# Row norms applied in the transposes by a diagonal, and low parts taken from PSUM, in a one-core hybrid attention and recurrence step

## The chip, the core and the metric

The kernel runs on one core of a Trainium2 chip, as one launch. The core has five engines that run at once, each with its own queue of instructions, and wait for each other by semaphores: TensorE (PE, matrix products, whose weight loads the profile lists apart as PEld), VectorE (DVE), ScalarE (ACT), GpSimd (POOL) and SyncE (SP, which issues most DMAs here). Matrix products take both operands from the on-chip memory SBUF and write to the accumulation memory PSUM, from which only DVE and ACT read in this kernel.

The metric is the device time of one execution in microseconds (us). "The time before" is the median of three runs.

## The reference

One layer of a diffusion backbone, on 1024 latent tokens and 256 context tokens of width 1024, in float32:

```python
def rms_norm(x, w):
    xf = x.astype(F32)
    y = xf * lax.rsqrt(jnp.mean(xf * xf, axis=-1, keepdims=True) + EPS)
    return (y * w.astype(F32)).astype(x.dtype)

def one_block(qi):                      # in block_attention
    s = jnp.einsum('bqkgd,bskd->bkgqs', qi, kf) * scale
    p = jax.nn.softmax(s, axis=-1)
    return jnp.einsum('bkgqs,bskd->bqkgd', p, vf)

def trunk_layer(x, mod, norm_mix_w, mix_w, ffn_w, ctx_k, ctx_v, s0_fwd, s0_bwd, latent):
    sh1, sc1, g1, sh2, sc2, g2 = mod
    h = rms_norm(x, norm_mix_w) * (1.0 + sc1) + sh1
    out, k, v, s = token_mixer(h, *mix_w, ctx_k, ctx_v, s0_fwd, s0_bwd, latent)
    x = x + g1 * out
    norm_ffn_w, w_ff1, w_ff2 = ffn_w
    h = rms_norm(x, norm_ffn_w) * (1.0 + sc2) + sh2
    x = x + g2 * (jnp.square(jax.nn.relu(h @ w_ff1)) @ w_ff2)
    return x, k, v, s
```

`token_mixer` multiplies `h` by `w_in` (1024 x 5376), runs attention (8 heads of 64, 2 key heads; latents attend to 1024 latent and 512 cached keys, context to itself) and a gated linear recurrence forward and backward (4 heads, chunks of 32), gates and merges the two and multiplies by `w_out`. Three places divide or multiply whole rows by one number for each row: the first RMSNorm, the softmax's sum, and the second RMSNorm. They are what the change touches.

## The kernel before

Tokens come in three tiles: t = 0 and 1 are the latents (512 each, four blocks of 128 rows), t = 2 is the context (256, two blocks). To keep float32 precision at the fast product rate, most operands are split into a high part (rounded to the reduced type float32r, by ACT) and a low part (the rest, by DVE), and a product is three fast ones: high x high, high x low, low x high (`mm3` L319 to L321, `z_tok` L336 to L338). Some products are ordinary float32 matmuls without a split, those of the recurrence among them (L1083, L1095, L1114, L1116).

The stages follow each other:

1. *Start* (up to about 100 us). `norm1_rows` (L229) loads rows, sums their squares, takes the reciprocal root (`rst`) and scales the rows in place (`scale`, L253, on DVE). `norm1_tr` (L259) transposes 128x128 blocks on PE with the identity into PSUM; `norm1_col` (L271 to L277) applies the modulation, which by now is one scale `sc` and one shift `sh` for each partition, and writes the high part `hi` (ACT) and the low part `lo` (DVE), by way of `xnb`. For every third column of t < 2 `xnb` is computed by DVE (L274), else by ACT (L276).
2. *Attention* (about 160 to 710 us), 32 units of 256 latent queries of one head with 1536 keys (6 steps each) and 8 of the context with 256 keys (1 step). A unit's `score` (L819) makes scores of 128 queries x 512 keys, `expo` (L830) the exponentials `pexp` and their sums, whose reciprocal is `rs` (L834), `norm` (L838) multiplies `pexp` by `rs`, turn about on POOL and DVE (`NORM`), `trans` (L860) transposes four 128x128 blocks of `pexp` into one PSUM tile, from which ACT takes the high part `pTh` and DVE the low part `pTl` (L863), and `value` (L874, L875) multiplies them by the values. `events` sets the order by due times in steps of a unit, and between events `fill` puts products of `w_in` (a `Filler`) on PE in proportion.
3. *Recurrence* (about 710 to 1010 us), `hgrn`: 24 units, each with `prep` (scans and scalings on DVE and POOL), `keys_t` (transposes, L1072), `scores` (L1083), `states_` (L1095), `out` (L1114, L1116). Products of `w_in` fill PE here as well. The columns of the modulation are made on the way: `ada_cols` (L176) multiplies, copies the result to SBUF (`ev`, L178), and leaves a rest `late` in a list `todo`: a transpose (L182), a sum `adas` (L185) and an addition (L186). The rest is run when the next group of `w_in` products has begun.
4. *Projections* (about 1010 to 1320 us). The outputs of both branches are projected, gated and merged, multiplied by `w_out`, and added to the rows `xrow`. `out_norm` (L1385) stores the rows, computes their norm and scales them in place on DVE; `norm2_t` (L1393) transposes them on PE.
5. *MLP* (the rest).

What sets the order: PE's instructions stand as the code writes them; on DVE, ACT, POOL and SP a scheduler orders them by its own estimate, with `tc.high_priority` and `tc.issue_after(x)` ("not before x in the order") as hints. On each engine instructions then run strictly in that order. Buffers come from rings by name (`RING_OF`): a ring's next tile waits for the readers of the one that had the buffer. The ring "K" has one buffer, which holds `ident0` at the start and `R`, a constant of the recurrence's scans, later.

## Time and profile before

| | |
|---|---|
| median of three runs | 2056.77 us (2056.67 to 2057.38) |
| profiled execution, its own time | 2056.44 us |
| its span in the profile | 2054.7 us |
| granted TensorE clock, mean | 0.998 |
| DVE busy | 1407.0 us, 68% |
| ACT busy | 941.1 us, 46% |
| POOL busy | 533.1 us, 26% |

How to read the rows of the profile: a row of a group has line, engine, operation, the tile written, the tiles read (for a product the moving one first), the shapes and the number of records; then the busy time, the mean duration in ns, and the idle time of the engine just before, with what ended it. In a row of the timeline stand start, duration of the merged instructions, engine, line, operation, tiles, shapes and count, and in brackets the idle time before and its releaser. A matmul's duration is its latency; matmuls overlap, so what one costs is read from starts. L12 is line 12 of the kernel.

### The profile page before, as it was taken

To read this page: it belongs to the slowest core of one execution; us is meant where nothing else is said; L and a number is where in the kernel's file an instruction comes from. 1 tells how busy PE (TensorE), PEld (TensorE's weight loads), DVE (VectorE), ACT (ScalarE), POOL (GpSimd) and SP (SyncE) were. 2 spreads that over 40 slices of the span, in tenths; PEclk is the share of its full clock that TensorE was granted. 3 is DMA by queue.
4 is the path that set the end of the run, shared out by engine and by line. 5 is a ranking of instruction groups with operands and counts; after the bars stand their busy time and mean duration, and the time that the engine had idled before them with its cause. 6 is when DMAs were issued, how large, how long until landed. Compare 5 with 4: busy or idle time off the path is not lost.

```text
span 2054.7 us, 33792 instructions
## 1 busy us (share of the span) xinstructions
PE 2013.7 (98%) x12470; PEld 1735.2 (84%) x12470; DVE 1407.0 (68%) x2733; ACT 941.1 (46%) x1973; POOL 533.1 (26%) x526
## 2 busy tenths in 40 slices
PE   7899999999999999999999999999999999999998
PEld 5698889988889978888888889988888888888886
DVE  5866776767776788879254635886666666577686
ACT  4634555555555423333321335755455544333443
POOL 1452233333333355545112101222122110000120
PEclk9999999999999999999999999999999999999999
DMA  9452220321212454554644533854444489455764
GB/s 318 160 189 78 70 83 32 104 88 55 77 50 80 132 176 158 165 168 158 199 136 149 179 113 119 253 184 152 159 146 157 145 292 361 147 160 175 232 238 142
DMA packets 220612, 317.38 MB, mean 154 GB/s; under 512 B 18760, under 2 KB 139808, under 8 KB 220448
## 3 DMA queue, kind: packets, MB, share of 16 engines
q1 hardware_dynamic: 207968, 275.32, 41.8%
q0 software_dynamic: 12480, 39.91, 5.2%
q8 instruction: 98, 1.61, 0.3%
q14 instruction: 66, 0.54, 0.1%
HBM read 229.43 MB, written 85.74 MB: 153 GB/s over the span
## 4 chain that ended last, share of the span: by engine, by line
PE 87%; DVE 6%; DMA 3%; ACT 2%; issue 1%; SPq 0%; POOL 0%; POOLq 0%; DVEq 0%; ACTq 0%
PE ps_g L319 8%; PE ps_g L321 7%; PE ps_g L320 7%; PE ps_s L819 4%; PE ps_t L860 4%; PE ps_g L1749 2%; PE ps_g L1748 2%; PE ps_g L1750 2%; PE ps_s L1593 2%; PE ps_s L1594 2%; PE ps_s L1595 2%; PE ps_g L875 2%; PE ps_s L1748 2%; PE ps_s L1749 2%; PE ps_s L1750 2%; PE ps_g L336 2%
## 5 line engine op out<-in xcount | busy, mean ns | idle before, releaser
L319 PE MATMUL ps_g<-hs,wsp 128*128 128x512 f32 (+1 forms) x896 | 322.5, 360 | 4.0 <-DVE adas L185 4.0
L321 PE MATMUL ps_g<-hs,wsp 128*128 128x512 f32 (+1 forms) x896 | 309.6, 345 | 0.0
L320 PE MATMUL ps_g<-hs,wsp 128*128 128x512 f32 (+1 forms) x896 | 309.3, 345 | 0.0
L838 POOL TENSOR_SCALAR pexp<-pexp,rs 128x512 f32<-128x512 f32 (+1 forms) x104 | 169.4, 1635 | 367.0 <-ACT pTh L863 174.4
L286 ACT ACTIVATE wsp<-wraw 128x512 fp32r<-128x512 f32 (+1 forms) x186 | 116.7, 667 | 228.6 <-PE ps_g L320 90.8
L287 DVE TENSOR_TENSOR wsp<-wraw,wsp 128x512 fp32r<-128x512 f32 (+1 forms) x186 | 147.0, 812 | 98.2 <-ACT wsp L286 97.7
L319 PEld LDWEIGHTS ps_g<-hs,wsp 128*128 128x128 f32 x896 | 169.9, 190 | 24.9 <-issue 4.6
L321 PEld LDWEIGHTS ps_g<-hs,wsp 128*128 128x128 f32 x896 | 169.5, 189 | 21.6
L863 ACT ACTIVATE pTh<-ps_t 128x512 fp32r<-128x512 f32 x200 | 118.6, 603 | 143.8 <-PE ps_t L860 142.4
L320 PEld LDWEIGHTS ps_g<-hs,wsp 128*128 128x128 f32 x896 | 170.2, 190 | 15.0
L286 ACT ACTIVATE ah<-ar 128x640 fp32r<-128x640 f32 (+1 forms) x112 | 80.9, 723 | 186.5 <-PE ps_g L1749 102.3
L820 DVE TENSOR_REDUCE mx<-ps_s 128x1 f32<-128x512 f32 (+1 forms) x208 | 137.2, 663 | 41.6 <-PE ps_s L819 40.7
L830 ACT ACTIVATE pexp<-ps_s,ngm 128x512 f32<-128x512 f32 (+1 forms) x208 | 137.5, 670 | 36.0 <-DVE ngm L824 35.2
L863 DVE TENSOR_TENSOR pTl<-ps_t,pTh 128x512 fp32r<-128x512 f32 x200 | 135.4, 680 | 18.0 <-ACT pTh L863 17.8
L287 DVE TENSOR_TENSOR ah<-ar,ah 128x640 fp32r<-128x640 f32 (+1 forms) x112 | 91.9, 821 | 77.0 <-ACT ah L286 75.8
L819 PE MATMUL ps_s<-Kl,Ql 128*128 128x512 f32 (+1 forms) x416 | 131.0, 412 | 1.0 <-ACT pexp L830 0.9
L860 PE MATMUL ps_t<-ident,pexp 128*128 128x128 f32 x800 | 121.4, 273 | 4.3 <-DVE pexp L838 3.0
L336 PE MATMUL ps_g<-wsp,hs 128*128 128x256 f32 x400 | 115.9, 290 | 0.0
L338 PE MATMUL ps_g<-wsp,hs 128*128 128x256 f32 x400 | 112.9, 282 | 0.0
L337 PE MATMUL ps_g<-wsp,hs 128*128 128x256 f32 x400 | 112.6, 281 | 0.0
L875 PE MATMUL ps_g<-pTl,Vl 128*128 128x256 f32 x400 | 105.4, 286 | 3.6 <-DVE pTl L863 3.5
L860 PEld LDWEIGHTS ps_t<-ident,pexp 128*128 128x128 f32 x800 | 93.7, 140 | 16.2 <-DVE pexp L838 4.6
(422 smaller groups left out, 5379.1 us busy)
## 6 DMA issues: line engine op xcount, KB each, us to landing
ar<-AF SPq DMA_DIRECT2D x112, 320.0 KB, 3.3
wraw<-in_w_ff SPq DMA_DIRECT2D x32, 1024.0 KB, 6.2
wr<-in_w_ff SPq DMA_DIRECT2D x128, 256.0 KB, 4.3
wraw<-in_w_in SPq DMA_DIRECT2D x18, 1024.0 KB, 5.6
wraw<-in_w_ada SPq DMA_DIRECT2D x16, 1024.0 KB, 5.7
AF<-a POOLq DMA_DIRECT2D x48, 256.0 KB, 2.8
AF<-t POOLq DMA_DIRECT2D x48, 256.0 KB, 2.3
wa<-in_w_ada SPq DMA_DIRECT2D x32, 256.0 KB, 6.0
```

The costliest lines, as they stand in the source:

```text
L286: s_.activation(hi, raw, AF.Copy)
L287: return v.tensor_tensor(lo, raw, f32(hi), op=ALU.subtract)
L319: pe.matmul(out, hi[:, k, :], mh, start=(first and k == 0), stop=False)
L320: pe.matmul(out, hi[:, k, :], ml, start=False, stop=False)
L321: pe.matmul(out, lo[:, k, :], mh, start=False, stop=(last and k == kcs - 1))
L336: pe.matmul(po[:, bb, :], mh[:, off:off + P], wh[:, k % 4, :], start=(k == 0), stop=False)
L819: pe.matmul(pq[:, 0:n], self.qh[:, q0:q0 + P], K[self.g][var][self.kts[i]], start=(var == 0), stop=(var == 1))
L830: s_.activation(e[:, 0:n], self.ps.pop((j, i))[:, 0:n], AF.Exp, bias=self.mx[j], accum_out=self.sm[j][:, i:i + 1])
L838: NORM[(i + j) % len(NORM)].tensor_scalar(x, x, self.rs[j], None, op0=ALU.mult)
L860: pe.transpose(pt[:, a, j * P:(j + 1) * P], self.Ps[j][i][:, b * P:(b + 1) * P], ident)
L863: behind[:] = s_.activation(hi, pt, AF.Copy), v.tensor_tensor(lo, pt, f32(hi), op=ALU.subtract)
L875: pe.matmul(pv[:, 0:256], V[self.g][kg][:, b, :], lo[:, a, :], start=False, stop=(k == last))
```

## The change

Three places that scaled rows now leave the rows as they are and put the factors on the diagonal of a 128x128 matrix, the identity times one number for each row (`dg`, `dgo`). The transpose with the identity becomes a product with that diagonal, which transposes and scales at once. It is no longer issued as a transpose but as an ordinary float32 matmul, with the same stationary operand (the block of rows) and the diagonal as the moving one. This is done for the latent tiles in `norm1_tr` (t < 2; the context tile keeps its scaling and transposes), for all of attention in `trans`, and for all ten row blocks in `norm2_t`. The diagonals of the start and of attention are four slots of one tile in the ring "K"; those of the output rows lie in buffers that are no longer read (masks, `hnb`, `ada_l`, and one new).

Further, for every third column of a latent tile the low part is computed from PSUM as (x * sc - hi) + sh in place of (x * sc + sh) - hi. And at the start of the recurrence the rest of the last modulation columns is run before the loop, and the first unit prepared in the loop is put behind its sum `adas`.

```diff
@@ -37,3 +37,3 @@
-    "ze": "I", "ident0": "K",
+    "ze": "I", "ident0": "K", "dg": "K",
@@ -114,2 +114,3 @@
     ident = f32(ident_r)
+    DG = {"n": 0, "t": S((P, 4, P), name="dg")}
     cols = cp.tile([P, 104], F32, name="cols")
@@ -170,2 +171,4 @@
 
+    adas = [None]
+
     def ada_cols(pa, raw, ci):
@@ -184,3 +187,3 @@
             with tc.high_priority(offset=600):
-                v.tensor_reduce(x.rearrange("p (c r) -> p c r", c=2), pt.rearrange("p (i c x) -> p c x i", i=2, c=2)[:, :, 0:2, :], axis=AX.X, op=ALU.add)
+                adas[0] = v.tensor_reduce(x.rearrange("p (c r) -> p c r", c=2), pt.rearrange("p (i c x) -> p c x i", i=2, c=2)[:, :, 0:2, :], axis=AX.X, op=ALU.add)
             v.tensor_tensor(modc[:, :, ci:ci + 2], x.rearrange("p (c r) -> p r c", c=2),
@@ -250,2 +253,7 @@
         def scale(i):
+            if t < 2:
+                if i == 0:
+                    for b in blocks:
+                        v.tensor_scalar(DG["t"][:, b], ident, rst[:, b - b0:b - b0 + 1], None, op0=ALU.mult)
+                return
             for b in blocks:
@@ -258,3 +266,7 @@
         for b in blocks or range(NB[t]):
-            pe.transpose(pt[:, b * P:(b + 1) * P], xs[b][kc // 4][:, (kc % 4) * P:(kc % 4 + 1) * P], ident)
+            out, x = pt[:, b * P:(b + 1) * P], xs[b][kc // 4][:, (kc % 4) * P:(kc % 4 + 1) * P]
+            if t < 2:
+                pe.matmul(out, x, DG["t"][:, b], start=True, stop=True)
+            else:
+                pe.transpose(out, x, ident)
         return pt
@@ -273,6 +285,7 @@
             if kc % 3 == 1 and t < 2:
-                v.tensor_scalar(xn, pt, sc, sh, op0=ALU.mult, op1=ALU.add)
+                v.scalar_tensor_tensor(xn, pt, sc, f32(hi), op0=ALU.mult, op1=ALU.subtract)
+                low[0] = v.tensor_scalar(lo, xn, sh, None, op0=ALU.add)
             else:
                 s_.activation(xn, pt, AF.Identity, scale=sc, bias=sh)
-            low[0] = v.tensor_tensor(lo, xn, f32(hi), op=ALU.subtract)
+                low[0] = v.tensor_tensor(lo, xn, f32(hi), op=ALU.subtract)
         return made
@@ -811,3 +824,3 @@
                 self.qh = q_at[self.h, self.t]
-                self.ps, self.mx, self.sm, self.rs = {}, {}, {}, {}
+                self.ps, self.mx, self.sm, self.rs, self.dg = {}, {}, {}, {}, {}
             if i == 0:
@@ -835,5 +848,7 @@
 
-        def norm(self, j, i):
-            x = self.Ps[j][i][:, 0:KG[self.kts[i]]]
-            NORM[(i + j) % len(NORM)].tensor_scalar(x, x, self.rs[j], None, op0=ALU.mult)
+        def diag(self, j):
+
+            DG["n"] += 1
+            self.dg[j] = DG["t"][:, DG["n"] % 4]
+            v.tensor_scalar(self.dg[j], ident, self.rs[j], None, op0=ALU.mult)
 
@@ -844,3 +859,3 @@
                 out += [(a + 1, self.expo, (j, i)) for a, j, i in ev]
-                out += [(a + 2, self.norm, (j, i)) for a, j, i in ev]
+                out += [(a + 2, self.diag, (j,)) for a, j, i in ev]
             else:
@@ -848,3 +863,3 @@
                 out += [(a, self.expo, (j, i)) for (j, i), a in zip(self.tasks, (-5.4, -4.9, -4.4, -2.4, -1.9, -1.4))]
-                out += [(a, self.norm, (j, i)) for (j, i), a in zip(self.tasks, (-4.35, -3.45, -2.45, -1.35, 0.1, 2.1))]
+                out += [(a, self.diag, (j,)) for j, a in ((0, -4.35), (1, -1.35))]
             for p2 in range(self.nstep):
@@ -859,3 +874,3 @@
                 for j in range(2):
-                    pe.transpose(pt[:, a, j * P:(j + 1) * P], self.Ps[j][i][:, b * P:(b + 1) * P], ident)
+                    pe.matmul(pt[:, a, j * P:(j + 1) * P], self.Ps[j][i][:, b * P:(b + 1) * P], self.dg[j], start=True, stop=True)
             hi = S((P, 2, 256), F32R, name="pTh")
@@ -888,3 +903,2 @@
 
-    NORM = [g_, v]
     gone, keyed, copied = [None], [None], [None]
@@ -1163,2 +1177,3 @@
         units[0].keys_t()
+        todo.pop()()
         for i in range(N + LATE):
@@ -1167,2 +1182,4 @@
                 with ExitStack() as after:
+                    if i == 0:
+                        after.enter_context(tc.issue_after(adas[0].ins))
                     after.enter_context(tc.issue_after(copied[0].ins))
@@ -1361,2 +1378,5 @@
     xrow = {}
+    dgo = [masks[0], masks[1], hnb] + [ada_l[:, k:k + 4].rearrange("p k c -> p (k c)") for k in (0, 4)]
+    dgo.append(cp.tile([P, P], F32, tag="s0", name="s0", bufs=2))
+    dgo = {b: dgo[b % 4 + (4 if b > 7 else 0)] for b in range(10)}
 
@@ -1384,3 +1404,3 @@
         rstd_of(rst[:, 0:1], ss[:, 2:3], 1, 1.0 / D)
-        v.tensor_scalar(xrow[b], xrow[b], rst[:, 0:1], None, op0=ALU.mult)
+        v.tensor_scalar(dgo[b], ident, rst[:, 0:1], None, op0=ALU.mult)
 
@@ -1392,3 +1412,3 @@
             kj, b = (kc, j) if t < 2 else (kc + j // 2, j % 2)
-            pe.transpose(pt[:, j, :], xrow[4 * t + b][:, kj * P:(kj + 1) * P], ident)
+            pe.matmul(pt[:, j, :], xrow[4 * t + b][:, kj * P:(kj + 1) * P], dgo[4 * t + b], start=True, stop=True)
         if t < 2:
```

How the instructions stand now, at the three places where the time is worked out. Names in brackets are the engines (or DMA queues) whose semaphores a row waits for; "x3" merges like rows.

PE in attention, at one step of `trans`, with the scores of a later unit and `value` behind it; before:

```order
L860 MATMUL ps_t<-ident,pexp 128x128 [waits DVE_49]
L860 MATMUL ps_t<-ident,pexp 128x128 x3
L819 MATMUL ps_s<-Kl,Ql 128x512 [waits Activation_49]
L819 MATMUL ps_s<-Kl,Ql 128x512
L874 MATMUL ps_g<-pTh,Vl 128x256 [waits Activation_49]
L875 MATMUL ps_g<-pTl,Vl 128x256
```

and with the change (L832, L889 and L890 are the old L819, L874 and L875):

```order
L875 MATMUL ps_t<-dg,pexp 128x128 [waits DVE_49]
L875 MATMUL ps_t<-dg,pexp 128x128 x3
L832 MATMUL ps_s<-Kl,Ql 128x512 [waits Activation_49]
L832 MATMUL ps_s<-Kl,Ql 128x512
L889 MATMUL ps_g<-pTh,Vl 128x256 [waits Activation_49]
L890 MATMUL ps_g<-pTl,Vl 128x256
```

The rows stand in the same order, four to a PSUM tile; the four are now matmuls with `dg` in the place of the identity.

DVE in attention, at the end of one unit's exponentials: the sum's reciprocal `rs`, and what follows it; before:

```order
L833 TENSOR_REDUCE rs<-sm 128x1 [waits Activation_49]
L834 RECIPROCAL rs<-rs 128x1 [waits DVE_49]
L838 TENSOR_SCALAR pexp<-pexp,rs 128x512 [waits DVE_49]
L838 TENSOR_SCALAR pexp<-pexp,rs 128x512
L863 TENSOR_TENSOR pTl<-ps_t,pTh 128x512 [waits Activation_49]
L820 TENSOR_REDUCE mx<-ps_s 128x1 [waits PE_49]
```

and with the change (L846, L847 and L878 are the old L833, L834 and L863):

```order
L846 TENSOR_REDUCE rs<-sm 128x1 [waits Activation_49]
L847 RECIPROCAL rs<-rs 128x1 [waits DVE_49]
L853 TENSOR_SCALAR dg<-ident,rs 128x128 [waits DVE_49]
L878 TENSOR_TENSOR pTl<-ps_t,pTh 128x512 [waits Activation_49]
L978 TENSOR_SCALAR ze<-ze,fc_1308,fc_1307 128x512 [waits DMAHW7_49,Activation_49]
L833 TENSOR_REDUCE mx<-ps_s 128x1 [waits PE_49]
```

The two multiplications of 128x512 weights have gone, with those that POOL had, and one diagonal of 128x128 stands there.

DVE at the start of the recurrence, around the preparation of the second unit (`ucp`, `usf`: its scans, L1008 and L1009) and the sum `adas` (L185); before:

```order
L1034 TENSOR_TENSOR uf<-usf,um 128x512 [waits Pool_49]
L980 SCALAR_TENSOR_TENSOR ze<-ze,ps_g 128x512 [waits Activation_49]
L1008 SCALAR_TENSOR_TENSOR ucp<-R,uf 128x512 [waits DMAHW0_49]
L1009 SCALAR_TENSOR_TENSOR usf<-uf,R 128x511 [waits DMAHW5_49]
L1010 MEMSET usf 128x1
...
L980 SCALAR_TENSOR_TENSOR ze<-ze,ps_g 128x512 [waits Activation_49]
L1034 TENSOR_TENSOR uf<-usf,um 128x512 [waits Pool_49]
L1012 SCALAR_TENSOR_TENSOR ucp<-R,uf 128x512 [waits DMAHW4_49]
...
L1044 TENSOR_TENSOR um<-um,ucp 128x4 [waits DVE_49]
L185 TENSOR_REDUCE adas<-ps_g 128x4 [waits PE_49]
L1104 SCALAR_TENSOR_TENSOR ust<-s_9203,udec,ps_s 128x128 [waits PE_49]
```

and with the change (L994, L1022 and L1023 are the old L980, L1008 and L1009, L188 and L189 the old L185 and L186):

```order
L1048 TENSOR_TENSOR uf<-usf,um 128x512 [waits Pool_49]
L994 SCALAR_TENSOR_TENSOR ze<-ze,ps_g 128x512 [waits Activation_49]
L300 TENSOR_TENSOR wsp<-wraw,wsp 128x512 [waits PE_49,Activation_49]
L300 TENSOR_TENSOR wsp<-wraw,wsp 128x512 [waits Activation_49]
L994 SCALAR_TENSOR_TENSOR ze<-ze,ps_g 128x512 [waits DMAHW1_49,Activation_49]
L188 TENSOR_REDUCE adas<-ps_g 128x4 [waits PE_49]
L1022 SCALAR_TENSOR_TENSOR ucp<-R,uf 128x512 [waits DMAHW0_49]
L1023 SCALAR_TENSOR_TENSOR usf<-uf,R 128x511 [waits DMAHW5_49]
L1024 MEMSET usf 128x1
L189 TENSOR_TENSOR modc<-adas,cols 128x2x2 [waits DVE_49]
```

The sum stood behind the preparation of the second unit and the beginning of the third's; now it stands just ahead of the second unit's scans, behind two low parts of weights (`wsp`) and an evacuation (`ze`) that stood later. On PE the transpose that it reads (L182, now L185) has moved from behind the first unit's scores to right behind that unit's own transposes, and the row at which PE waited for the PSUM bank (a L319 of 128x256) names DVE's semaphore before and only PE's own now.

## The prediction

> **What bounds the kernel now.** I read the page first: busy shares, then the chain that ended last, then the stages, and only then single groups.
>
> ```profile
> PE 2013.7 (98%) x12470; PEld 1735.2 (84%) x12470; DVE 1407.0 (68%) x2733; ACT 941.1 (46%) x1973; POOL 533.1 (26%) x526
> PEclk9999999999999999999999999999999999999999
> PE 87%; DVE 6%; DMA 3%; ACT 2%; issue 1%; SPq 0%; POOL 0%; POOLq 0%; DVEq 0%; ACTq 0%
> ```
>
> TensorE (PE) is busy 98% of the span, its clock is granted in full in every slice, and 87% of the chain that sets the end is PE. A busy PE is not yet a full PE, so I looked at how matmuls follow each other and at PE's idle time by stage.
>
> ```profile
> 50.00:100.00 50.00, 43.78 (x216) 33.96 (x214) 42.49 (x98) 33.81 (x82) 21.70 (x18) 1.00 0.48 156
> 160.00:710.00 550.00, 541.17 (x3940) 489.15 (x3939) 391.36 (x879) 312.05 (x751) 179.67 (x112) 1.00 0.24 76
> 710.00:1010.00 300.00, 296.01 (x2460) 252.81 (x2460) 232.40 (x554) 91.93 (x234) 148.84 (x156) 0.99 0.54 170
> 1210.00:1320.00 110.00, 109.65 (x724) 100.52 (x723) 66.89 (x128) 61.88 (x136) 15.55 (x21) 1.00 0.55 169
> ```
>
> Columns: stage, its length, then busy time and count of PE, of its weight loads (PEld), DVE, ACT and POOL. The attention stage (160 to 710) has PE idle for 8.8 of 550 us, the recurrence (710 to 1010) for 4.0 of 300, the part of the output projection where the rows are transposed (1210 to 1320) for 0.35 of 110. Only before 100 us is there much idle PE. So from 160 us on, a PE instruction added costs its full time, and one taken from another engine is worth only what PE idled for it.
>
> **What the change does on PE.** Attention's weights, the latent input tiles and the output rows went through TensorE as transposes with the identity moving; now they are ordinary float32 matmuls with a diagonal moving. The count stays the same. What an ordinary 128x128 float32 matmul costs is in this trace:
>
> ```profile
> L860 PE MATMUL ps_t<-ident,pexp 128*128 128x128 f32 x800 | 121.4, 273 | 4.3 <-DVE pexp L838 3.0 <-DVE pTl L863 1.1
> L259 PE MATMUL ps_t<-ident,xr 128*128 128x128 f32 x80 | 12.5, 282 | 5.6 <-ACT xnb L276 4.0 <-DVE xnb L274 0.8 <-DVE kT L287 0.5
> L1393 PE MATMUL ps_t<-ident,x 128*128 128x128 f32 x80 | 11.4, 273 | 0.3 <-ACT hx L1400 0.3
> L1095 PE MATMUL ps_s<-uv,ukt 128*128 128x128 f32 x160 | 22.0, 276 | 0.0
> L1116 PE MATMUL ps_s<-uv,usm 128*128 128x128 f32 x80 | 14.8, 275 | 0.0
> ```
>
> L860 is called 4 times for each of 200 PSUM tiles and shows x800: one record per transpose. L1095 and L1116 are ordinary float32 matmuls. L1116 is called once per 128-token block of each backward unit, (4+4+2) blocks x 4 heads = 40 calls, and shows x80; L1095 is called for all (4+4+4+4+2+2) x 4 = 80 blocks and shows x160. **An ordinary float32 matmul is two records, each with its own weight load**; a transpose is one. Now the time from one start to the next, first four transposes, then eight ordinary products:
>
> ```profile
> 702.31 0.28 PE L338 MATMUL ps_g<-wsp,hs 128*128 128x256 f32 x1
> 702.43 0.60 PE L860 MATMUL ps_t<-ident,pexp 128*128 128x128 f32 x4
> 702.78 0.36 PE L336 MATMUL ps_g<-wsp,hs 128*128 128x256 f32 x1
> 702.98 0.28 PE L337 MATMUL ps_g<-wsp,hs 128*128 128x256 f32 x1
> ```
> ```profile
> 772.07 0.38 PE L1114 MATMUL ps_s<-ust,uw 128*128 128x128 f32 x2
> 772.28 0.39 PE L1116 MATMUL ps_s<-uv,usm 128*128 128x128 f32 x2
> ...
> 773.62 0.39 PE L1116 MATMUL ps_s<-uv,usm 128*128 128x128 f32 x2
> 773.77 0.47 PE L319 MATMUL ps_g<-hs,wsp 128*128 128x512 f32 x1
> 774.08 0.39 PE L320 MATMUL ps_g<-hs,wsp 128*128 128x512 f32 x1
> ```
>
> Columns: start, duration of the merged rows, instruction and count. From 702.43 to 702.98 go four transposes and one 128x256 matmul (0.12 us, from 702.31 to 702.43): 0.43 us, 0.108 each. From 772.07 to 774.08 go 16 records and one 128x512 matmul (774.08 is the start after it; such a one takes 0.23 between starts): 1.78 us, 0.111 per record. So a transpose that becomes an ordinary product costs 2 x 0.111 - 0.108 = **0.115 us more** of PE. I take this, not the means of some 275 ns, which are latencies of overlapping instructions.
>
> The Trainium skill bears on this in "TensorE: Matmul & The Clock Gate", section "Terms", which says that the transpose mode is 4 times faster for FP32. By that a product would take 4 x 0.108 us, 944 of them 306 us more in all, an estimate of about 2350 us. This trace shows 2.06 times (0.222 against 0.108 us) and two records, not four.
>
> **Attention: +92.0, and -8 given back.** 800 x 0.115 = 92.0 us more on PE. In return 208 multiplications of 128x512 weights go, half on POOL and half on DVE, and 80 diagonals come, on DVE:
>
> ```profile
> L838 POOL TENSOR_SCALAR pexp<-pexp,rs 128x512 f32<-128x512 f32 (+1 forms) x104 | 169.4, 1635 | 367.0 <-ACT pTh L863 174.4 <-DVE rs L834 96.2 <-PE ps_t L860 35.1
> ...
> L838 DVE TENSOR_SCALAR pexp<-pexp,rs 128x512 f32<-128x512 f32 (+1 forms) x104 | 61.2, 613 | 1.6
> ```
> ```profile
> L758 DVE TENSOR_SCALAR hnb<-hnb 128x128 f32<-128x128 f32 x1 | 0.2, 227 | 1.0 <-DMA hnb<-in_hgrn_norm_w 1.0
> ```
> ```profile
> PE ps_g L875 <- DVE pTl L863: 3.5, 6, 1.0
> PE ps_t L860 <- DVE pexp L838: 3.0, 6, 1.1
> ...
> PE ps_t L860 <- DVE pTl L863: 1.1, 2, 0.9
> ...
> PE ps_s L819 <- ACT pexp L830: 0.9, 3, 0.5
> ```
>
> A diagonal is a 128x128 scalar multiplication from SBUF; the nearest row is L758, 0.227 us. DVE gets 61.2 - 80 x 0.227 = 43 us lighter, POOL 169. Neither is the bound (DVE 391 of 550 us), so all this buys is PE's waits. The last four rows have them (total, times, longest): 8.5 us in 17 waits. Waits for the weights (pexp, 3.0) lose their cause: the diagonal needs only the sum, as the first multiplication did before, and is one instruction of 0.2 us where POOL took 1.6 for each tile. The others (pTl on DVE, pexp on ACT) shrink since DVE is lighter and PE takes 17% longer per step. I take 8; the bounds are 0, if they only change their cause, and 12, since idle is counted from the modelled end, 0.27 us after a start where the next start could come after 0.11, which hides 0.16 in each of 17 waits. The new wait is that of a unit's first product for its diagonal. Behind the diagonal on DVE stand the low parts of the previous unit, for which PE waits too. But the diagonal's due time is 1.35 steps ahead of its first use, a step being 550 us / 200 = 2.7 us, so 3.7 us cover 0.23; without the cover it would cost up to 80 x 0.23 = 18.
>
> **Latent tiles at the start: +5.** 64 products x 0.115 = 7.4 us. Here PE isn't always the bound:
>
> ```profile
> 18.97 0.50 PE L618 MATMUL ps_s<-wraw,hs 128*128 128x512 f32 x1 [1.27 <-ACT hs L271]
> ...
> 33.24 0.63 PE L589 MATMUL ps_g<-wa,ada_l 128*32 128x128 f32 x12 [0.34 <-DMA wa<-in_w_ada]
> ...
> 50.62 0.72 PE L259 MATMUL ps_t<-ident,xr 128*128 128x128 f32 x4
> ...
> 60.30 0.66 PE L259 MATMUL ps_t<-ident,xr 128*128 128x128 f32 x4 [1.43 <-ACT xnb L276]
> ```
>
> It waits for ACT's first part (1.27 at 18.97), for a transfer (0.34 at 33.24), and for PSUM that ACT has not read (1.43 at 60.30; with its like 5.6 before L259). Added PE time ahead of such a wait vanishes in it: the 32 products of the second tile (3.7) mostly, those of the first hardly, since there ACT waits for PE. I count 3.4 of 7.4 as hidden; bounds 0 and all of it. The 16 multiplications that go save nothing: L253 is off PE's path. Six low parts (every third column) now start only after ACT's high part, not beside it: up to the high part's 0.78 us each, 4.7; nearer 0, as one wait for them is 0.8 in all; I take +1. One wait is new. The second tile's diagonals stand on DVE behind the scaling of hnb, which waits for its transfer:
>
> ```profile
> 49.86 1.84 DVE L253 TENSOR_SCALAR xr<-xr,rst 128x512 f32<-128x512 f32 x4 [0.52 <-DMA xr<-in_x_prompt]
> 52.73 0.23 DVE L758 TENSOR_SCALAR hnb<-hnb 128x128 f32<-128x128 f32 x1 [1.03 <-DMA hnb<-in_hgrn_norm_w]
> ```
>
> The scaling of rows ran at 49.86; the diagonals can't before 53. PE came for these tiles at 50.62 and will come 3.5 us later with the first tile's 32 products ahead, about 54. So it is covered by a microsecond; if not, it costs up to 2.5.
>
> **Start of the recurrence: -2.5.** Moving the last modulation transpose forward, and its sum ahead of the second unit's preparation, aims at one stall:
>
> ```profile
> 717.65 1.57 DVE L1008 TENSOR_TENSOR_SCAN ucp<-R,uf 128x512 f32<-128x512 f32 x1
> ...
> 719.85 0.28 ACT L178 ACTIVATE ev<-ps_g 128x128 f32<-128x128 f32 x1 [0.44 <-PE ps_g L176]
> ...
> 729.44 0.69 DVE L1034 TENSOR_TENSOR uf<-usf,um 128x512 f32<-128x512 f32 x1 [2.65 <-POOL usf L1025]
> ...
> 731.30 0.60 PE L1072 MATMUL ps_t<-ident,uf 128*128 128x128 f32 x4
> ...
> 733.58 0.39 PE L321 MATMUL ps_g<-hs,wsp 128*128 128x512 f32 x1
> ...
> 737.92 0.39 PE L319 MATMUL ps_g<-hs,wsp 128*128 128x256 f32 x1 [3.96 <-DVE adas L185]
> ```
>
> From 733.58 to 737.92 PE starts nothing, 4.1 us more than its pace of 0.23, until the sum (adas) leaves DVE's queue and frees a PSUM bank. In the new order the sum stands ahead, and PE waits there only for itself. What is late next: the unit's scans, at 717.65 before, must now follow the sum, which can't come before the copy on ACT (719.85 + 0.28), the transpose and the sum, some 720.7. So uf, ready at 730.1, comes at about 733, and the transposes that want it, which went at 731.30, wait some 1.6 us. Net -4.1 + 1.6 = -2.5; bounds -4 and +1 (if POOL's chain slips further). The buffer R now takes the diagonals' place and is filled after the last product; its first reader comes only after the last attention output, so I count nothing; without that cover it would be two POOL fills of about 1 us.
>
> **Output rows: +9.2.** 80 x 0.115 us, with 0.3 us of idle before L1393 to hide in. The ten multiplications (128x1024) that go waited for the rows' store, but no PE instruction waited for them: nothing.
>
> **The sum.** 92.0 - 8 + 5 - 2.5 + 9.2 = +95.7. The profiled execution took 2056.44 us (span 2054.7), 0.3 below the median of the runs shown, so 2056.4 + 95.7 = **2152 us**. Bounds together: 92 - 12 + 0 - 4 + 8.9 = +85 (2141) and 92 + 0 + 14.6 + 1 + 9.2 = +117 (2173).
>
> **Rivals.**
> 1. *Nothing comes back.* The waits only move, with the diagonal's own wait behind DVE's queue: +92 + 9 + 9 + up to 18, 2166 to 2185. For it: the low parts still stand on DVE. Against it: 43 us less on DVE. Chance 0.07.
> 2. *The extra records hide.* If what limits PE in attention were the weights' path through DVE, POOL and ACT, a third of the 92 would fit in: about 2121. Against it: 541 of 550 us busy and matmuls at a steady pace. Chance 0.06.
> 3. *Four records per product*, high and low halves of both operands: 944 x (4 x 0.111 - 0.108) = +317, less some 5 given back, about 2368. L1095 and L1116 have the same shape and type and show two: 0.02. The Trainium skill's factor of four, above, would come out near it.
> 4. *The other side: one record per product.* If the product with a diagonal were issued like a transpose, its price would be 0.003 x 944 = +3, and the waits given back (8 + 2.5 + about 2) would decide: about 2047, faster. It turns where a product's extra falls below 12.5 / 944 = 0.013 us; the rows say 0.115. For it only that the count of calls doesn't change. Chance 0.02.
> That the change doesn't do what it says I give nothing of its own: every multiplication is gone from the new order.
>
> **How the numbers follow.** The forecast's own case has 0.83, around 2152. The range reaches from 2139 to 2168: the sum's bounds without the last corner above (0.04 of the forecast's own case). Outside are that, most of rival 1 (0.05) and rivals 2 to 4 (0.10), not quite 2 in 10. Faster by over 0.2% (4 us, about what a measurement of this kernel can tell from no change): 0.02, rival 4. Within 0.2%: 0.01. Slower: 0.97.
>
> **What would show it.** Right: the attention product with x1600 records and the stage about 84 us longer; those of the start with x128 and of the output rows with x160; PE idle in attention below 3 us; POOL down by some 169 us; no 4 us stop near the recurrence's start, but one of 1 to 2 us before its second transposes. Wrong: x800 or x3200 records, or a new wait of PE for dg on DVE.

## The result, and the profile after

| | before | with the change |
|---|---|---|
| device time, median (lowest to highest) | 2056.76 us (2056.67 to 2057.38, 4 runs) | 2146.45 us (2145.33 to 2147.01, 4 runs) |
| ratio to before, 95% interval | 1 | 1.0432 (1.0419 to 1.0445) |
| span of the profiled execution | 2054.7 us | 2143.1 us |
| granted TensorE clock, mean | 0.998 | 0.999 |

The changed kernel is 4.3% slower. The forecast was 2152 us with a range of 2139 to 2168. The page of the changed kernel, busy time by engine, and the shares of the chain that ended last:

```profile
PE 2112.3 (99%) x13414; PEld 1846.5 (86%) x13414; DVE 1370.1 (64%) x2701; ACT 946.2 (44%) x1973; POOL 364.2 (17%) x422
...
PE 94%; DVE 2%; DMA 1%; ACT 1%; issue 1%; POOL 0%; SPq 0%; POOLq 0%; ACTq 0%; DVEq 0%
```

PE has 944 records more (13414 against 12470), one for each transpose that became a product. POOL is 168.9 us lighter and DVE 36.9, and the time is longer all the same: neither was what the end waited for. The groups of the changed products (busy time, mean of one, idle before):

```profile
L875 PE MATMUL ps_t<-dg,pexp 128*128 128x128 f32 x1600 | 211.2, 275 | 0.3 <-DVE dg L853 0.3
...
L269 PE MATMUL ps_t<-dg,xr 128*128 128x128 f32 x128 | 16.8, 280 | 1.5 <-ACT xnb L289 1.3 <-DVE xnb L286 0.3
...
L1413 PE MATMUL ps_t<-mask,x 128*128 128x128 f32 x64 | 9.7, 274 | 0.0
...
L1413 PE MATMUL ps_t<-ada_l,x 128*128 128x128 f32 x48 | 9.3, 274 | 0.0
...
L1413 PE MATMUL ps_t<-hnb,x 128*128 128x128 f32 x32 | 6.2, 275 | 0.0
...
L1413 PE MATMUL ps_t<-s,x 128*128 128x128 f32 x16 | 3.1, 275 | 0.0
```

800, 64 and 80 calls show 1600, 128 and 64 + 48 + 32 + 16 = 160 records: two for each. The mean of one is the latency and is nearly that of a transpose before (273 ns); what differs is the number of records. The stages, in stretches that hold the same work as those of the prediction (attention, recurrence, output rows; length, then busy PE, PEld, DVE, ACT, POOL, then the clock):

```profile
167.80:794.00 626.20, 625.47 (x4740) 583.70 (x4739) 361.28 (x855) 316.25 (x751) 10.96 (x10) 1.00 0.20 67
794.00:1089.20 295.20, 294.41 (x2460) 251.75 (x2459) 235.31 (x554) 92.07 (x234) 148.37 (x156) 1.00 0.54 173
1289.20:1407.80 118.60, 118.60 (x799) 109.74 (x798) 64.87 (x129) 64.23 (x138) 15.41 (x21) 1.00 0.48 157
```

Attention takes 626.2 us where it took 550, and PE is idle in it for 0.7 us. The recurrence takes 295.2 in place of 300. PE's waits, of the whole span (total, times, longest):

```profile
...
PE ps_s L631 <- ACT hs L283: 4.3, 3, 2.8
PE ps_t L271 <- DVE qT L300: 2.0, 2, 1.7
...
PE ps_s L1109 <- issue: 0.8, 1, 0.8
...
PE ps_s L832 <- ACT pexp L843: 0.5, 1, 0.5
...
PE ps_t L875 <- DVE dg L853: 0.3, 1, 0.3
```

The waits for weights and low parts in attention are gone, as is the 4 us for `adas`. The products wait for a diagonal once, 0.3 us. The waits that grew are the first two rows, both at the start of the program: for `hs` 4.3 us in place of 1.7, now with one stop of 2.8, and for `qT` 2.0 in place of 0.3.

For the terms of the sum I took the same landmarks in both traces (the start of a given PE instruction) and their distance. Figures in us:

| stretch | forecast | measured |
|---|---|---|
| start, to the last transpose of the front (91.4, now 99.2) | +5.0 | +7.8 |
| attention, to its last transpose (702.8, now 786.8) | +84.0 | +76.2 |
| recurrence, to its last scores (989.1, now 1068.4) | -2.5 | -4.8 |
| output rows, first to last transpose | +9.2 | +8.6 |
| the rest | 0 | +0.7 |
| span | +95.7 | +88.5 |

### The profile page after: what moved, and what is told of

The parts are those of the page before. It is cut to its first block, busy times and chain, and to the rows that moved or that the text cites. A ratio compares the mean times of both kernels' runs of the same rounds, so it can differ in the third digit from the quotient of the medians.

```text
span 2143.1 us, 35315 instructions
## 1 busy us (share of the span) xinstructions
PE 2112.3 (99%) x13414; PEld 1846.5 (86%) x13414; DVE 1370.1 (64%) x2701; ACT 946.2 (44%) x1973; POOL 364.2 (17%) x422
## 4 chain that ended last, share of the span: by engine, by line
PE 94%; DVE 2%; DMA 1%; ACT 1%; issue 1%; POOL 0%; SPq 0%; POOLq 0%; ACTq 0%; DVEq 0%
PE ps_t L875 8%; PE ps_g L332 8%; PE ps_g L334 8%; PE ps_g L333 8%; PE ps_s L832 4%; PE ps_g L890 2%; PE ps_g L349 2%; PE ps_g L351 2%; PE ps_g L889 2%; PE ps_g L350 2%; PE ps_g L1769 2%; PE ps_g L1770 2%; PE ps_g L1768 2%; PE ps_s L1615 2%; PE ps_s L1614 2%; PE ps_s L1613 2%
## 5 line engine op out<-in xcount | busy, mean ns | idle before, releaser
L833 DVE TENSOR_REDUCE mx<-ps_s 128x1 f32<-128x512 f32 (+1 forms) x208 | 138.6, 668 | 125.2 <-PE ps_s L832 124.8
L878 ACT ACTIVATE pTh<-ps_t 128x512 fp32r<-128x512 f32 x200 | 119.7, 600 | 213.6 <-PE ps_t L875 212.8
L875 PE MATMUL ps_t<-dg,pexp 128*128 128x128 f32 x1600 | 211.2, 275 | 0.3 <-DVE dg L853 0.3
L875 PEld LDWEIGHTS ps_t<-dg,pexp 128*128 128x128 f32 x1600 | 199.6, 191 | 6.8 <-issue 0.8
L878 DVE TENSOR_TENSOR pTl<-ps_t,pTh 128x512 fp32r<-128x512 f32 x200 | 136.5, 683 | 10.0 <-ACT pTh L878 9.6
L832 PE MATMUL ps_s<-Kl,Ql 128*128 128x512 f32 (+1 forms) x416 | 130.4, 412 | 0.5 <-ACT pexp L843 0.5
L996 POOL TENSOR_TENSOR ze<-ze,hnb 128x512 f32<-128x512 f32 x10 | 14.2, 1424 | 633.0 <-DVE ze L994 326.8
L889 PE MATMUL ps_g<-pTh,Vl 128*128 128x256 f32 x400 | 103.8, 281 | 0.0
```

Of the source, the lines that this page charges most:

```text
L832: pe.matmul(pq[:, 0:n], self.qh[:, q0:q0 + P], K[self.g][var][self.kts[i]], start=(var == 0), stop=(var == 1))
L875: pe.matmul(pt[:, a, j * P:(j + 1) * P], self.Ps[j][i][:, b * P:(b + 1) * P], self.dg[j], start=True, stop=True)
L878: behind[:] = s_.activation(hi, pt, AF.Copy), v.tensor_tensor(lo, pt, f32(hi), op=ALU.subtract)
L889: pe.matmul(pv[:, 0:256], V[self.g][kg][:, b, :], hi[:, a, :], start=(k == 0), stop=False)
```

## The experiments

Eleven further kernels ran, one of them under two labels; "before" beside them had medians of 2056.71 to 2057.26 us. Differences of times below are to that of the same chip; "by the landmarks" means distances between the same PE instructions in two profiles.

**Attention alone.** The kernel before, with `diag`, its events and the product in `trans`, nothing else.

> The kernel before with the attention part of the change alone (diagonals and ordinary products in place of 208 multiplications and 800 transposes). Theory A (the stages add up, and the attention stage of the changed kernel, 76.2 us longer from first to last transpose, is all of this part's doing): 2056.4 + 76 = 2132 to 2133 us. Rival (the later orders made part of it: the recurrence or the start shifted the load): off by more than 4 us.

Measured: 2135.16 us (2132.98 to 2136.47), ratio 1.0376 (1.0361 to 1.0392), which is +78.5 us and 2 us above theory A's figure and less than the 4 us of the rival. By the landmarks attention is +76.3 us, as in the changed kernel, so that stage is all of this part's doing. The rest of this profile's difference lies in stages that the edit doesn't touch (front +1.7, recurrence +0.8, behind the output rows +0.7), where the other profiles scatter as well.

**Recurrence alone.** The kernel before, with these lines (`adas[0]` is the sum of L185):

```diff
         units[0].keys_t()
+        todo.pop()()
...
+                    if i == 0:
+                        after.enter_context(tc.issue_after(adas[0].ins))
```

> The kernel before with the two edits at the start of the recurrence alone. Theory A (the 4.1 us stop goes, and what comes late next costs less than a microsecond, as the recurrence of the changed kernel is 4.8 us shorter between landmarks): 2051.5 to 2053 us. Rival (the 4.8 us came from lighter DVE and POOL queues at the end of attention, and the edits alone only move the stop, as my -2.5 had it with 1.6 us given back): 2054 to 2056 us.

Measured: 2052.45 us (2051.02 to 2053.83, 10 runs), ratio 0.9977 (0.9968 to 0.9986), recurrence -4.9 us by the landmarks, as theory A had it. One run more of the same kernel, under a label that names another one, gave 2051.41 us, inside what was expected:

> The kernel before with the recurrence part of the change alone, again, as the base of comparison on this chip: 2051.0 to 2053.8.

This part is a gain, inside a change that loses.

**Products without diagonals, and diagonals' gain without products.** The first keeps all 208 multiplications and only issues the 800 transposes as products with the identity. The second keeps the transposes and leaves out the multiplications by the row norms, so its weights are not normalised.

```diff
-                    pe.transpose(pt[:, a, j * P:(j + 1) * P], self.Ps[j][i][:, b * P:(b + 1) * P], ident)
+                    pe.matmul(pt[:, a, j * P:(j + 1) * P], self.Ps[j][i][:, b * P:(b + 1) * P], ident, start=True, stop=True)
```
```diff
-                out += [(a + 2, self.norm, (j, i)) for a, j, i in ev]
...
-                out += [(a, self.norm, (j, i)) for (j, i), a in zip(self.tasks, (-4.35, -3.45, -2.45, -1.35, 0.1, 2.1))]
```

> The kernel before with all 208 multiplications kept, and the 800 transposes of attention issued as ordinary products with the identity. It pays for the second record and saves no multiplication. Theory A (the waits that went in the changed kernel went because the multiplications went): +92 less at most 4, 2144 to 2149 us, PE still waiting for pexp on DVE. Theory B (they went because PE takes 17% longer for each step, so that DVE and ACT get ahead): the same 2131 to 2135 us as the attention part with diagonals.

> The kernel before without the 208 multiplications of the attention weights by the reciprocal sums (the weights are left unnormalised), transposes as before. Theory A (the multiplications made the waits): the 12 us of waits that went in the changed kernel go here too, 2044 to 2047 us. Theory B (PE's slower step made them go): only the waits for pexp go, 4 us, 2051 to 2053 us.

Measured: the first 2134.62 us (2132.98 to 2135.42), ratio 1.0376 (1.0362 to 1.0390), attention +76.9; the second 2046.01 us (2045.30 to 2046.95), ratio 0.9947 (0.9933 to 0.9960), attention -11.2. PE's waits in attention, of the first:

```profile
PE ps_s L819 <- ACT pexp L830: 0.5, 1, 0.5
PE ps_t L860 <- DVE pexp L838: 0.5, 1, 0.5
```

and of the second:

```profile
PE ps_t L858 <- DVE pTl L861: 0.7, 1, 0.7
PE ps_s L819 <- ACT pexp L830: 0.6, 2, 0.5
PE ps_s L819 <- DMA Kl<-KS: 0.3, 1, 0.3
```

Before had 8.5 us here, and 1.0 and 1.6 are left. With the multiplications still there but slower transposes, nearly all of the waits are gone; with the multiplications gone and the old transposes, too. So either cause is enough. In the changed kernel the longer PE work alone already covers the multiplications, and taking them away buys 0.6 us at most: +76.9 with them, +76.3 without.

**One record per product.** The attention part once more, with the weights and the diagonal in float32r (the weights are rounded to that format):

```diff
-                e = self.Ps[j][i] = S(name="pexp")
+                e = self.Ps[j][i] = S(dt=F32R, name="pexp")
...
+    DG = {"n": 0, "t": S((P, 4, P), dt=F32R, name="dg")}
```

> The kernel before with the attention part of the change alone, the weights and the diagonal written as float32r, so that a product is one record as a transpose is (the weights are rounded to that format). Theory A (the price of the change is the second record of each product, and nothing else): x800 records of about 0.11 us, the attention stage about 11 us shorter than before, as without any multiplication, 2045 to 2048. Theory B (a moving diagonal that is made per row block, and its reading in place of the kept identity, costs something of its own): attention between +0 and +76 us, 2057 to 2133.

Measured: 2052.52 us (2051.22 to 2053.79, 10 runs), ratio 0.9977 (0.9968 to 0.9986), attention -6.4. The group:

```profile
L863 PE MATMUL ps_t<-dg,pexp 128*128 128x128 f32 x800 | 113.9, 264 | 2.2 <-DVE dg L841 1.3 <-DVE pTl L866 0.7
```

800 records, and the 76 us are gone. The price of the change is the second record. The time lies between the two theories' figures, as far from the one as from the other (4.5 us): 4.8 us of attention less came back than without multiplications (-6.4 against -11.2), of which the row names 2.2 as idle, 1.3 of it for the diagonals; where the other 2.6 lie isn't shown. With PE this fast, the wait for `dg` that was named as a risk appears.

**The start.** Three kernels: diagonal products alone, the new low parts alone, both.

```diff
-            pe.transpose(pt[:, b * P:(b + 1) * P], xs[b][kc // 4][:, (kc % 4) * P:(kc % 4 + 1) * P], ident)
...
+                pe.matmul(out, x, DG["t"][:, b], start=True, stop=True)
```
```diff
-                v.tensor_scalar(xn, pt, sc, sh, op0=ALU.mult, op1=ALU.add)
+                v.scalar_tensor_tensor(xn, pt, sc, f32(hi), op0=ALU.mult, op1=ALU.subtract)
+                low[0] = v.tensor_scalar(lo, xn, sh, None, op0=ALU.add)
...
```

> The kernel before with the diagonal products of the latent start alone (64 transposes, 12 of the multiplications on x), low parts as before. Theory A (7.4 us of records, 3.4 of them hidden, plus 2.8 of the changed order of DVE, and the low parts cost 1): the last transpose of the front starts 6.5 to 7 us later than before, 2063 to 2064. Theory B (the low parts are what made the start longer than forecast): 4 us later, about 2061.

> The kernel before with the low parts from PSUM alone, norms and transposes of the start as before. Theory A (the form of the low parts itself is worth about a microsecond either way, and its 5 us beside the products came from the order): 2056 to 2058.5. Theory B (the form saves VectorE and ScalarE time that PE waits for): 2052 to 2055.

> The kernel before with the start's part of the change whole: diagonal products and the low parts from PSUM. Theory A (the 12.8 us of the products alone came from the order in which VectorE then stood, and the new form of the low parts brings another order and shorter VectorE work): the last transpose of the front starts 7 to 8.5 us later than before, as in the whole change, and 2064 to 2066. Theory B (the 12.8 us belong to the products themselves, and the whole change came out lower by something in the other parts): 2069 to 2071.

Measured, with the front's landmark: products alone 2070.09 us (2069.59 to 2070.80), ratio 1.0063 (1.0049 to 1.0076), +12.8; low parts alone 2060.22 us (2058.65 to 2063.43, 10 runs), 1.0018 (1.0009 to 1.0027), +3.5; both 2066.37 us (2065.24 to 2067.26), 1.0046 (1.0032 to 1.0059), +9.8. Neither theory named the first two times; the third lies 0.4 us above theory A, and its landmark above the 8.5 that A allowed. The parts don't add: 12.8 + 3.5 is not 9.8. What differs is where DVE's queue is waited for. The timelines of PE with the products alone, and with the low parts alone:

```profile
91.30 0.69 PE L269 MATMUL ps_t<-ident,xr 128*128 128x128 f32 x2 [3.24 <-DVE qT L297]
```
```profile
83.44 0.44 PE L259 MATMUL ps_t<-ident,xr 128*128 128x128 f32 x2 [3.23 <-DVE qT L288]
```

In each the transposes of the front wait 3.2 us for the low part of `qT`, which DVE has behind other work of the query's preparation. Before that wait was 0.3 us in all; with both parts it is 2.0, the longest 1.7, as in the changed kernel. And the clock fell behind a stop (length, busy PE, PEld, DVE, ACT and POOL, clock), with the products alone twice, with both once:

```profile
32.60:36.80 4.20, 4.14 (x11) 3.30 (x12) 1.39 (x2) 2.01 (x4) 0.00 (x0) 0.59 1.10 350
...
91.20:93.20 2.00, 1.90 (x6) 1.61 (x7) 0.50 (x3) 1.02 (x2) 0.00 (x0) 0.50 0.38 131
93.20:95.20 2.00, 2.00 (x8) 1.58 (x7) 0.30 (x1) 0.00 (x0) 0.00 (x0) 0.71 0.03 8
```
```profile
32.30:37.20 4.90, 4.79 (x21) 3.55 (x24) 1.39 (x2) 2.07 (x4) 0.00 (x0) 0.65 1.11 353
```

At 0.59 for 4.2 us, 0.41 x 4.2 = 1.7 us are lost, at 0.50 and 0.71 another 1.6, at 0.65 for 4.9 again 1.7. Without the clock, if its loss reaches the landmark whole, the products alone are +9.5, and both parts +8.1, near the +7.8 of the whole change, whose profile shows 1.00 there. With the low parts alone the clock fell as well, to 0.50 from 20.4 to 23.8 us. How much of that is in its +3.5 isn't shown: with POOL alone multiplying, below, it fell at the same place, and the landmark lies only 0.3 us after that of before.

**The splits put later.** The changed kernel, with the splits of later weight rows issued behind the columns' work:

```diff
-            front_w(kc + 2)
-            front_w(kc + 3)
+            for k in (kc + 2, kc + 3):
+                raw = w_load(k)
+                with tc.issue_after(made.ins if made else scales.ins):
+                    split(*w_row(k), raw)
```

> The changed kernel, with the splits of weight rows 4 to 7 of the front (high and low part) issued behind the column work of the step before, so that the scale of the next columns no longer stands behind a low part that waits for a weight row from memory. Theory A (the start came out at +7.8 and not at +5 because of that order): the stop of 2.78 us before the second pair's products is gone, the last transpose product of the front starts 2 to 3 us earlier (96 to 97 us instead of 99.2), time 2143.2 to 2144.6. Theory B (TensorE would have waited there anyway, for the weight rows themselves or for the norms): the stop moves to another tile, less than 1 us comes back, 2145.5 to 2146.5.

Measured: 2144.74 us (2143.64 to 2145.99, 5 runs), ratio 1.0427 (1.0412 to 1.0441). The interval overlaps that of the change, so the times don't settle it. The trace says more. The stop of 2.8 us is gone: the products of L602 behind it start 2.5 us sooner than in the changed kernel (33.22 against 35.70). Then comes a stop that the changed kernel hasn't (PE's waits):

```profile
PE ps_s L637 <- DVE hs L287: 1.2, 1, 1.2
```

and its cause, DVE's timeline:

```profile
41.89 0.69 DVE L242 SCALAR_TENSOR_TENSOR sqv<-xr 128x512 f32<-128x512 f32 x1 [2.55 <-DMA xr<-in_x_sample]
42.51 0.08 DVE L242 DVE_READ_ACCUMULATOR sqv<-xr 128x1 f32 x1
42.51 0.48 DVE L287 TENSOR_SCALAR hs<-xnb,modc 128x512 fp32r<-128x512 f32 x1
```

A sum of squares that waits for its transfer now stands ahead of the low part `hs`. In the end 0.3 us of the front came back, as theory B had it, though the time lies between the two theories: one instruction that waits for memory went from the head of DVE's queue, and another took its place. The rest of the 1.7 us between the two medians is in the profiles behind the output rows (1.4), where the kernels are alike.

**Faster than both.** The recurrence part with one-record products, and the recurrence part with transposes as before and all multiplications on POOL:

```diff
-    NORM = [g_, v]
+    NORM = [g_]
```

> The recurrence part of the change and the attention part with one-record products (weights and diagonals in float32r), neither the start nor the output rows. If the two gains lie in different stages and add, as the landmarks say (-4.3 and -4.7 us): 2047 to 2049.5, faster than before and than either alone. Rival: the recurrence part's gain is a share of the same stops and does not add, 2051 to 2053.

> The recurrence part of the change, with transposes as before and all 208 multiplications of the weights on GpSimd (1.63 us each, some 340 us of a stage of 535) in place of half on each. Theory A (the stops in attention are those of VectorE's low parts, which stand behind its multiplications): attention 6 to 11 us shorter, 2042 to 2047. Theory B (GpSimd's longer multiplication is itself late for the transposes): attention longer by 5 us or more, 2057 or above.

Measured: 2047.08 us (2046.06 to 2049.67), ratio 0.9954 (0.9941 to 0.9966), and 2047.46 us (2045.93 to 2053.88), ratio 0.9962 (0.9949 to 0.9975). The first adds as expected. The second lies half a microsecond above its range; attention is 6.1 us shorter, and what PE waits for there, from 175 us on, is now POOL (one more such stop of 1.8 us stands at the stage's beginning):

```profile
PE ps_t L862 <- POOL pexp L840: 3.3, 4, 1.3
PE ps_g L877 <- DVE pTl L865: 0.2, 1, 0.2
```

The waits for DVE's low parts (3.5 and 1.1 us before) are down to 0.2, so they were indeed the low parts that stood behind DVE's multiplications. Moving those to POOL, which was busy for 180 of the stage's 550 us, gives about half of what leaving them out gives (11.2), without a record more on PE. Of the two, this one rounds nothing.

## Why the prediction was right, and where its sizes were off

The mechanism was the one forecast, and the sum came out 7.2 us too high (88.5 of span, not 95.7). Attention was 7.8 us too high. That the total is off by no more than that is luck in part: the start's miss of +2.8 and the recurrence's of -2.3 about cancel. By its steps:

**The price of a product: right.** Between starts, records of L875 lie 0.112 us apart (median). Summed over the stage, the time that goes to these rows, start to next start, is 162.8 us now and 72.0 in the kernel without multiplications, where the row has hardly a stop: 90.8 for 800, or 0.1135 each, against 0.115 forecast. The one-record run shows that nothing else carries it. Rivals 2 to 4 fall by the count of records and by the +76: the records neither hid, nor were four, nor one. Rival 1 falls by what came back and by the single wait of 0.3 us for a diagonal. The Trainium skill, "TensorE: Matmul & The Clock Gate", section "Terms", has the transpose mode 4 times faster for FP32; this case shows about 2, 0.222 against 0.108 us.

**Attention's give-back: -8 forecast, 14.6 measured (90.8 - 76.2), outside its bounds of 0 and 12.** The step that failed is the upper bound, built on the list of waits with 8.5 us and 0.16 for each. That list holds only idle time after a modelled end. Counted from start to start, stops of over 0.12 us beyond the pace were some 13 us before (12.4 or 13.7, by how the pace of a kind of product is taken) and are some 1 now (0.4 or 2.0), about 12 of the 14.6; the rest is spread over shorter delays that I didn't assign. The reason given was also incomplete: I had the waits for the weights go because the multiplications went, and the others shrink because DVE is lighter and PE slower. The experiment with identity products gives back nearly as much (90.8 - 76.9 = 13.9) with every multiplication in place. So PE's longer steps are enough for nearly all of it; leaving out the multiplications gives 11.2 by itself; the change has both. A diagonal took 0.299 us, not 0.227; PE waited for one once, 0.3 us.

**Start: +5 forecast, +7.8 measured.** The term left out the place of the scale of columns 2 and 3 (`s`, L615) in DVE's queue. The changed kernel's timeline, DVE, then ACT, then PE:

```profile
30.37 0.69 DVE L300 TENSOR_TENSOR wsp<-wst,wsp 128x512 fp32r<-128x512 f32 x1 [2.97 <-ACT wsp L299]
30.98 0.17 DVE L614 TENSOR_TENSOR modc<-ps_g,cols 128x8 f32<-128x8 f32 x1
31.06 0.69 DVE L300 TENSOR_TENSOR wsp<-wst,wsp 128x512 fp32r<-128x512 f32 x1
31.67 0.16 DVE L615 SCALAR_TENSOR_TENSOR s<-modc,cols 128x4 f32<-128x4 f32 x1
...
29.71 1.32 ACT L299 ACTIVATE wsp<-wst 128x512 fp32r<-128x512 f32 x2 [2.87 <-DMA wst<-in_w_in]
31.92 0.78 ACT L283 ACTIVATE hs<-ps_t,modc,s 128x512 fp32r<-128x512 f32 x1 [0.89 <-DVE s L615]
...
32.75 0.50 PE L631 MATMUL ps_s<-wraw,hs 128*128 128x512 f32 x1 [2.78 <-ACT hs L283]
```

and before, DVE:

```profile
25.85 0.17 DVE L601 TENSOR_TENSOR modc<-ps_g,cols 128x8 f32<-128x8 f32 x1
26.05 0.17 DVE L602 SCALAR_TENSOR_TENSOR s<-modc,cols 128x4 f32<-128x4 f32 x1
```

Read it from the bottom: PE waits for `hs`, `hs` for the scale, the scale for a low part ahead of it in the queue, that for ACT, and ACT for the weight row, which lands at 29.7. Before, the scale went ahead of those low parts, at 26.05. This order stood in the new program and the prediction left it out; it weighed only the wait behind `hnb`, and that one was covered as said. The stop of 2.8 us is as large as the miss. That it is the cause of the whole 2.8 isn't settled: with the stop removed, 2.5 came back at the place and was lost again before the end of the front. The landmark itself is also no finer than that: in the eight profiles of kernels whose start isn't edited it lies at 91.7 to 93.8 us, 0.3 to 2.4 after the 91.4 of before. The size of the low parts' own term (+1) can't be had apart from the order either: +3.5 alone, -3.0 beside the products (-1.4 without the clock).

**Recurrence: -2.5 forecast, -4.8 measured.** Two things were missing. First, the wait of 1.6 us before the second transposes didn't come. The scans did start later, as worked out (805.10 less the shift of 84.0 is 721.1, against 717.65). But POOL's order had changed too; its timeline, with DVE's and PE's, in the changed kernel:

```profile
805.18 2.21 POOL L996 TENSOR_TENSOR ze<-ze,hnb 128x512 f32<-128x512 f32 x1 [1.14 <-DVE adas L188]
809.31 1.33 POOL L1039 TENSOR_TENSOR usf<-uf,usf 128x512 f32<-128x512 f32 x1 [1.92 <-ACT uf L1038]
...
813.86 0.69 DVE L1048 TENSOR_TENSOR uf<-usf,um 128x512 f32<-128x512 f32 x1
...
815.43 0.60 PE L1086 MATMUL ps_t<-ident,uf 128*128 128x128 f32 x4
```

and before, POOL:

```profile
726.87 1.28 POOL L982 TENSOR_TENSOR ze<-ze,hnb 128x512 f32<-128x512 f32 x1 [1.30 <-DVE ze L980]
728.11 1.29 POOL L1025 TENSOR_TENSOR usf<-uf,usf 128x512 f32<-128x512 f32 x1
```

Before, `usf` stood behind a `ze` that waited for DVE, and `uf` on DVE idled 2.65 us for it. Now that `ze` is done well before, `usf` ends 2.8 us earlier by the same landmark (810.6 - 84.0 against 729.4), and this slack takes up the later scans: the transposes go 84.1 us after their old time, no later than everything else.

Second, the stop of 4 us had a price beyond its length. The kernel before, right behind it (same columns, the clock is third from the end):

```profile
737.90:739.90 2.00, 1.98 (x27) 1.74 (x31) 2.00 (x6) 0.00 (x0) 1.04 (x1) 0.71 0.49 187
739.90:741.90 2.00, 2.00 (x22) 1.59 (x14) 1.97 (x5) 0.00 (x0) 0.56 (x1) 0.50 0.02 6
741.90:743.90 2.00, 2.00 (x18) 2.00 (x17) 2.00 (x2) 0.23 (x1) 1.49 (x2) 0.93 0.71 211
```

At these clocks 0.58 + 1.00 + 0.14 = 1.7 us are lost. 4.1 + 1.7, less a new stop before L1109 of 0.8 to 0.95, is about 4.9.

**Output rows: +9.2 forecast, +8.6 measured**, within what the bounds allowed.

## What to carry to other kernels

Moving a multiplication into a transpose is only free if the transpose stays one record: look at the count of records before the durations, since the mean latency of both is the same 0.27 us. Where PE is 98% busy, put elementwise work on whichever engine has room (here POOL, -6 us in attention) rather than on PE. And when an edit removes instructions from a queue, read the new order of every queue, POOL's and DVE's too, for an instruction that waits for memory and now stands ahead of one that PE needs.

## What the runs showed of the hardware beside

After a stop of PE the granted clock can fall to half. In the profiles with the 4.3 to 4.4 us stop at the recurrence's start (before, attention alone, identity products, no multiplications, one record), it was 0.50 for at least one of the next three stretches of 2 us. The Trainium skill, "TensorE: Matmul & The Clock Gate", section "What's actually happening", says that the clock goes to half after at least one idle window of some 3.4 us; these stops agree with that. But it also fell to 0.59, 0.65 and 0.50 behind stops of 2.6, 2.2 and 3.2 us in the two kernels of the start above, and not behind the stops of 2.8 us in the changed kernel and 3.2 us with the low parts alone, where it stayed at 1.00. Even one and the same stop does both: PE waits 1.27 us for the first `hs` at 18.97 us in the kernel before and at 19.71 with all multiplications on POOL, and behind it stand, first before, then with POOL:

```profile
20.00:23.40 3.40, 3.40 (x62) 2.76 (x64) 2.30 (x4) 0.78 (x2) 0.00 (x0) 1.00 1.09 360
```
```profile
20.00:23.40 3.40, 3.40 (x9) 2.67 (x9) 2.68 (x4) 1.51 (x3) 0.00 (x0) 0.50 1.09 359
```

So in these runs a stop can be shorter than 3.4 us and half clock follow; what decides it there they don't show. A stop of 4 us cost 1.7 us more than its length in the kernel before, and 2.9 with attention alone, where the three stretches stood at 0.50, 0.50 and 0.57.
